# A row-gradient kernel: each store issued when the preceding store has landed, with semaphores by Tile

## Chip, cores, metric

One core of one Trainium2 chip. The metric is the device time of one execution in microseconds.

## The reference

The input is 8192 x 8192 float32, the output has the same shape:

```python
def reference(x: np.ndarray) -> np.ndarray:
    return np.gradient(x, axis=1)
```

Inside a row the result is half the difference of the right and left neighbour; at each row's two ends it is the plain difference of two neighbours. 268.44 MB must be read and as much written, with next to no arithmetic.

## The kernel before

The rows are cut into 32 sets of 256 rows (two rows per partition, 64 KB per partition, 8.39 MB per set). Three slots in SBUF hold sets in turn. For each set GpSimd computes the row ends (128x4), VectorE the inner part in place (one pass of 17.2 us), ScalarE puts the row ends in, and the set is stored. All loads and stores are issued by SyncE on one queue. Below, S_i is the store of set i and L_i its load.

```python
with tc.tile_critical():
    ...                                   # semaphores: ld[k], st[k] per slot, and others
    def load(i):
        k = i % NB                        # NB = 3
        ...
            nc.sync.wait_ge(st[k], 16 * st_n[k])       # slot free: S_(i-3) has landed
            parts = [(ld[k], 0, R)] if i < nsets - 1 else [(ld_rows[r], r, 1) for r in range(R)]
        for sem, r0, nr in parts:
            nc.sync.dma_start(out=slots[k][...], in_=x_sets[i, ...]).then_inc(sem, 16)
    ...
    def work(i, r0, nr, ready, placer, storer, sem):
        ...                               # VectorE pass, then the row ends by `placer`
        storer.wait_ge(*at)               # the set is ready
        storer.dma_start(out=out_sets[i, ...], in_=b[...]).then_inc(sem, 16)

    for i in range(NB):
        load(i)
    for i in range(nsets):
        ...                               # put_aside (row ends) and work for set i
        if i > 0 and i - 1 + NB < nsets:
            load(i - 1 + NB)              # L_(i+2), after S_i on the queue
    ...                                   # wait for all stores
```

So the queue carries L0 L1 L2 S0 S1 L3 S2 L4 S3 L5 ... The last set is loaded and worked on in two halves.

Some words used below: every transfer is shared out over 16 DMA engines, and each engine has its own share of the queue, its *ring*. A ring that runs empty is called dry. A transfer has *landed* when all 16 shares are done. A *turn* is the place where a load gives way to a store or a store to a load. *Tile* is the part of the kernel language that can place semaphores by itself.

## Time and profile before

| | before |
|---|---|
| median of 3 runs | 1251.41 us |
| span in the profile | 1249.5 us |
| share of the DMA queue | 99.5% |
| VectorE busy | 551.7 us, 44% |
| packets alone: (7936 x 2.418 + 512 x 1.213) / 16 | 1238.1 us |

Read it from the bottom: a transfer is cut into packets of 64 KB, each carried by one of 16 engines; if every packet took its usual time (2.418 us, or 1.213 us for a half packet) and no engine ever paused, the packets alone would take 1238.1 us. A packet that takes more than its usual time is called *long*; "long packets sum to" means the time above the usual, as the mean of the 16 engines.

### The profile page before, as it was taken

To read this page: it belongs to the slowest core of one execution; us is meant where nothing else is said; L and a number is where in the kernel's file an instruction comes from. 1 tells how busy PE (TensorE), PEld (TensorE's weight loads), DVE (VectorE), ACT (ScalarE), POOL (GpSimd) and SP (SyncE) were. 2 spreads that over 40 slices of the span, in tenths; PEclk is the share of its full clock that TensorE was granted. 3 is DMA by queue.
4 is the path that set the end of the run, shared out by engine and by line. 5 is a ranking of instruction groups with operands and counts; after the bars stand their busy time and mean duration, and the time that the engine had idled before them with its cause. 6 is when DMAs were issued, how large, how long until landed. Compare 5 with 4: busy or idle time off the path is not lost.

```text
span 1249.5 us, 225 instructions
## 1 busy us (share of the span) xinstructions
DVE 551.7 (44%) x35; ACT 7.4 (1%) x32; POOL 6.8 (1%) x37
## 2 busy tenths in 40 slices
DVE  2851455324553345533455333554335543355550
ACT  0000000000000000000000000000000000000000
POOL 0000000000000000000000000000000000000000
DMA  9999999999999999999999999999999999999997
GB/s 403 436 436 418 428 430 436 434 430 436 432 436 434 436 434 432 432 432 420 434 436 432 434 436 432 436 434 436 436 430 436 436 434 422 428 436 436 436 434 330
DMA packets 9505, 536.88 MB, mean 430 GB/s; under 512 B 1056, under 2 KB 1056, under 8 KB 1056
## 3 DMA queue, kind: packets, MB, share of 16 engines
q1 hardware_dynamic: 9504, 536.88, 99.5%
q14 instruction: 1, 0.01, 0.0%
HBM read 268.44 MB, written 268.44 MB: 430 GB/s over the span
## 4 chain that ended last, share of the span: by engine, by line
another core or an unknown queue 78%; DMA 15%; DVE 3%; POOL 0%; issue 0%; ACT 0%; SPq 0%
DMA slot<-in_x_dram 9%; DMA out_dram<-slot 7%; DVE slot L100 3%; POOL ends L82 0%; ACT slot L114 0%; DVE slot L114 0%; SPq L165 0%; SPq L42 0%
## 5 line engine op out<-in xcount | busy, mean ns | idle before, releaser
L100 DVE CUSTOM_DVE_ANT_0 slot<-slot 128x16382 f32<-128x16382 f32 (+1 forms) x33 | 551.3, 16707 | 666.5 <-POOL ends L82 666.5
L114 ACT COPY slot<-ends 128x4 f32<-128x4 f32 x31 | 6.1, 198 | 1179.8 <-DVE slot L100 1179.8
L82 POOL TENSOR_TENSOR ends<-slot 128x4 f32<-128x4 f32 (+1 forms) x33 | 6.6, 199 | 1202.2 <-DMA slot<-in_x_dram 1202.2
L114 ACT ACT_TABLE_LOAD x1 | 1.3, 1283 | 0.9 <-SPq L42 0.9
L114 DVE COPY slot<-ends 128x2 f32<-128x2 f32 x2 | 0.3, 170 | 0.1
L154 POOL MEMSET const-bfloat16-1.0<- 128x1 bf16 x1 | 0.1, 102 | 0.0
L154 POOL MEMSET const-uint8-127<- 128x1 uint8 x1 | 0.1, 102 | 0.0
L154 POOL MEMSET const-float32-0.0<- 128x1 f32 x1 | 0.1, 99 | 0.2 <-issue 0.2
L154 POOL MEMSET const-float32-1.0<- 128x1 f32 x1 | 0.1, 99 | 0.0
## 6 DMA issues: line engine op xcount, KB each, us to landing
slot<-in_x_dram SPq DMA_DIRECT2D x2, 4096.0 KB, 52.9
out_dram<-slot SPq DMA_DIRECT2D x2, 4096.0 KB, 29.5
slot<-in_x_dram SPq DMA_DIRECT2D x31, 58.4
out_dram<-slot SPq DMA_DIRECT2D x31, 40.3
```

Source lines behind the costliest of these rows:

```text
L82: nc.gpsimd.tensor_sub(out=ends[:, i, r0 : r0 + nr, :], in0=xin[:, :, 1 : m : m - 2], in1=xin[:, :, 0 : m - 1 : m - 2],),
L100: nc.vector._custom_dve(dve_ops.TENSOR_TENSOR_REDUCE_SUB_MAX, out=mid, in0=after, in1=before, s0=0.0, s1=0.5,),
L114: at = done(copy(out=to, in_=of), placed[placer])
L154: nc = _bacc.Bacc("TRN2", target_bir_lowering=False, num_devices=1)
```

## The change

Intent: a store is not put on the queue before the preceding store has landed, so that it goes "behind a load that has begun", with the load for the slot just freed right behind it. Beside that the hand-made semaphores in a critical section give way to Tile's, the row ends are placed by VectorE and GpSimd in place of ScalarE, and the last set is loaded in one piece (still worked on and stored in halves). The core of the diff, with cuts:

```diff
-    with tc.tile_critical():
-        ld = [nc.alloc_semaphore(f"ld{k}") for k in range(NB)]
...
+    with tc.manual_schedule():
...
-            placer.wait_ge(*at)
-            copy = nc.scalar.copy if placer is nc.scalar else nc.vector.tensor_copy
-            at = done(copy(out=to, in_=of), placed[placer])
-            storer.wait_ge(*at)
-            storer.dma_start(...).then_inc(sem, 16)
+                placer = nc.gpsimd if i % 5 in (1, 3) and not last else nc.vector
+                ins = placer.tensor_copy(out=res[:, :, 0 : m : m - 1], in_=ends[:, i, r : r + nr, :])
+                placed = chain(i, ins, halved)        # chain: keep only the named dependencies
+                ins = nc.sync.dma_start(out=out_sets[i, ...], in_=b[...])
+                stores[i] = chain(i, ins, placed)
+                if 2 <= i and not last:
+                    tc.add_manual_dep(ins.ins, stores[i - 1].ins.name, landed, reason="behind a load that has begun")
...
-            if i > 0 and i - 1 + NB < nsets:
+            if 1 <= i and i - 1 + NB < nsets:
                 load(i - 1 + NB)
```

More of the change, by code (lines that the diff above doesn't have):

```diff
@@ L40 @@
     ends = pool.tile([P, nsets, R, 2], f32, name="ends", tag="ends")
-    with tc.tile_critical():
-        ld = [nc.alloc_semaphore(f"ld{k}") for k in range(NB)]
-        st = [nc.alloc_semaphore(f"st{k}") for k in range(NB)]
-        ld_rows = [nc.alloc_semaphore(f"ld_row{r}") for r in range(R)]
-        st_rows = [nc.alloc_semaphore(f"st_row{r}") for r in range(R)]
-        aside = [nc.alloc_semaphore("aside"), 0]
-        halved = [nc.alloc_semaphore("halved"), 0]
-        placed = {
-            nc.vector: [nc.alloc_semaphore("placed_dve"), 0],
-            nc.scalar: [nc.alloc_semaphore("placed_act"), 0],
-        }
-        def done(ins, counter):
-            ins.then_inc(counter[0])
-            counter[1] += 1
-            return counter[0], counter[1]
-        ld_n, st_n = [0] * NB, [0] * NB
-        def load(i):
-            k = i % NB
-            if i < NB:
-                parts = [(ld[k], 0, R)]
-            else:
-                nc.sync.wait_ge(st[k], 16 * st_n[k])
-                parts = [(ld[k], 0, R)] if i < nsets - 1 else [(ld_rows[r], r, 1) for r in range(R)]
-            for sem, r0, nr in parts:
-                nc.sync.dma_start(
-                    out=slots[k][:, SH + r0 * m : SH + (r0 + nr) * m],
-                    in_=x_sets[i, :, r0 * m : (r0 + nr) * m],
-                ).then_inc(sem, 16)
-            ld_n[k] += 1
-        def put_aside(i, r0, nr, sem, count):
-            k = i % NB
-            xin = slots[k][:, SH + r0 * m : SH + (r0 + nr) * m].rearrange("p (t m) -> p t m", m=m)
-            nc.gpsimd.wait_ge(sem, count)
-            return done(
-                nc.gpsimd.tensor_sub(
-                    out=ends[:, i, r0 : r0 + nr, :],
-                    in0=xin[:, :, 1 : m : m - 2],
-                    in1=xin[:, :, 0 : m - 1 : m - 2],
-                ),
-                aside,
-            )
-        def work(i, r0, nr, ready, placer, storer, sem):
-            b = slots[i % NB]
-            c0, c1 = r0 * m + 1, (r0 + nr) * m - 1
-            mid = b[:, c0:c1]
-            after = b[:, SH + c0 + 1 : SH + c1 + 1]
-            before = b[:, SH + c0 - 1 : SH + c1 - 1]
-            nc.vector.wait_ge(*ready)
-            at = done(
-                nc.vector._custom_dve(
-                    dve_ops.TENSOR_TENSOR_REDUCE_SUB_MAX,
-                    out=mid,
-                    in0=after,
-                    in1=before,
-                    s0=0.0,
-                    s1=0.5,
-                ),
-                halved,
-            )
-            res = b[:, r0 * m : (r0 + nr) * m].rearrange("p (t m) -> p t m", m=m)
-            to, of = res[:, :, 0 : m : m - 1], ends[:, i, r0 : r0 + nr, :]
-            placer.wait_ge(*at)
-            copy = nc.scalar.copy if placer is nc.scalar else nc.vector.tensor_copy
-            at = done(copy(out=to, in_=of), placed[placer])
-            storer.wait_ge(*at)
-            storer.dma_start(
-                out=out_sets[i, :, r0 * m : (r0 + nr) * m],
-                in_=b[:, r0 * m : (r0 + nr) * m],
-            ).then_inc(sem, 16)
@@ new lines, with chain @@
+    landed = mybir.DependencyInfo(mybir.DependencyClass.Sync, mybir.DependencyReason.DATA)
+    loads, stores = [], [None] * nsets
+    in_front = {}
+    def chain(i, ins, *needed):
+        group, engine = f"slot{i % NB}", ins.ins.engine
+        keep = [o.ins for o in needed]
+        if in_front.get(engine, (None,))[0] == group:
+            keep.append(in_front[engine][1])
+        tc.declare_no_dep(ins.ins, group=group, keep=keep, reason="implied by the needed step")
+        tc.add_to_no_dep_group(group, ins.ins)
+        in_front[engine] = group, ins.ins
+        return ins
@@ L121, with load @@
+    def load(i):
+        b = slots[i % NB]
+        ins = nc.sync.dma_start(out=b[:, SH : SH + W], in_=x_sets[i])
+        loads.append(chain(i, ins, *([stores[i - NB]] if i >= NB else [])))
+    with tc.manual_schedule():
         for i in range(NB):
@@ L123 @@
         for i in range(nsets):
-            k = i % NB
-            if i < nsets - 1:
-                ready = put_aside(i, 0, R, ld[k], 16 * ld_n[k])
-                work(i, 0, R, ready, nc.scalar, nc.sync, st[k])
-                st_n[k] += 1
-            else:
-                for r in range(R):
-                    ready = put_aside(i, r, 1, ld_rows[r], 16)
-                    work(i, r, 1, ready, nc.vector, nc.sync, st_rows[r])
-            if i > 0 and i - 1 + NB < nsets:
+            b = slots[i % NB]
+            xin = b[:, SH : SH + W].rearrange("p (t m) -> p t m", m=m)
+            ins = nc.gpsimd.tensor_sub(
+                out=ends[:, i, :, :],
+                in0=xin[:, :, 1 : m : m - 2],
+                in1=xin[:, :, 0 : m - 1 : m - 2],
+            )
+            at = [chain(i, ins, loads[i])]
+            last = i == nsets - 1
+            nr = 1 if last else R
+            for r in range(0, R, nr):
+                c0, c1 = r * m + 1, (r + nr) * m - 1
+                ins = nc.vector._custom_dve(
+                    dve_ops.TENSOR_TENSOR_REDUCE_SUB_MAX,
+                    out=b[:, c0:c1],
+                    in0=b[:, SH + c0 + 1 : SH + c1 + 1],
+                    in1=b[:, SH + c0 - 1 : SH + c1 - 1],
+                    s0=0.0,
+                    s1=0.5,
+                )
+                halved = chain(i, ins, *at)
+                res = b[:, r * m : (r + nr) * m].rearrange("p (t m) -> p t m", m=m)
+                placer = nc.gpsimd if i % 5 in (1, 3) and not last else nc.vector
+                ins = placer.tensor_copy(out=res[:, :, 0 : m : m - 1], in_=ends[:, i, r : r + nr, :])
+                placed = chain(i, ins, halved)
+                ins = nc.sync.dma_start(
+                    out=out_sets[i, :, r * m : (r + nr) * m], in_=b[:, r * m : (r + nr) * m]
+                )
+                stores[i] = chain(i, ins, placed)
+                if 2 <= i and not last:
+                    tc.add_manual_dep(ins.ins, stores[i - 1].ins.name, landed, reason="behind a load that has begun")
+                at = [halved]
+            if 1 <= i and i - 1 + NB < nsets:
                 load(i - 1 + NB)
-        for r in range(R):
-            nc.sync.wait_ge(st_rows[r], 16)
-        for k in range(NB):
-            nc.sync.wait_ge(st[k], 16 * st_n[k])
 _INS = ['x']
```

## The prediction

> **What bounds the kernel now.** I read the page first: the slices, the DMA queues and the busy shares.
>
> ```profile
> DVE 551.7 (44%) x35; ACT 7.4 (1%) x32; POOL 6.8 (1%) x37
> ...
> DMA  9999999999999999999999999999999999999997
> GB/s 403 436 436 418 428 430 436 434 430 436 432 436 434 436 434 432 432 432 420 434 436 432 434 436 432 436 434 436 436 430 436 436 434 422 428 436 436 436 434 330
> ...
> q1 hardware_dynamic: 9504, 536.88, 99.5%
> HBM read 268.44 MB, written 268.44 MB: 430 GB/s over the span
> ```
>
> The compute engines are idle for more than half of the span; the one DMA queue keeps the 16 engines at work for 99.5% of it, and the rate hardly leaves 420 to 436 GB/s. The bytes are the least that the task allows (the input once, the output once). So the bound is the transfer rate. 536.87 MB at the best slices' 436 GB/s is 1231.4 us; the span is 1249.5. All that any change of order can win lies in those 18 us.
>
> To split the 18 us I read the packet records. A full packet (64 KB, 8 of them per engine in each 8.39 MB transfer) takes 2.418 us in more than nine of ten cases; 7936 of those and 512 half packets of 1.213 us, over 16 engines, are 1238.1 us. What is above that: 2.5 us before the first packet and 1.8 us from the last packet to the end of the span; on the engine that ends last 7.9 us of packets longer than their 2.418 us, on the ten least hurt only about 2 us. The rest is gaps of some 0.1 us per engine in all: **no DMA engine ever runs dry**. The long packets are 0.6 us in the first load, 1.1 us in the last packet of the third load, where the first store follows, and then some 0.1 to 0.7 us in the last packet of most loads on six of the sixteen engines, dying out after 816 us. They sit where a load gives way to a store.
>
> The second view is the timeline of two steady sets (start, length, what was issued or run):
>
> ```profile
> 138.57 0.33 SPq L116 DMA_DIRECT2D out_dram<-slot  x1
> 140.43 0.34 SPq L70 DMA_DIRECT2D slot<-in_x_dram  x1
> 159.97 0.20 POOL L82 TENSOR_TENSOR ends<-slot 128x4 f32<-128x4 f32 x1 [38.91 <-DMA slot<-in_x_dram]
> 160.20 17.23 DVE L100 CUSTOM_DVE_ANT_0 slot<-slot 128x16382 f32<-128x16382 f32 x1 [21.89 <-POOL ends L82]
> 177.46 0.20 ACT L114 COPY slot<-ends 128x4 f32<-128x4 f32 x1 [38.92 <-DVE slot L100]
> 177.68 0.33 SPq L116 DMA_DIRECT2D out_dram<-slot  x1
> 179.28 0.34 SPq L70 DMA_DIRECT2D slot<-in_x_dram  x1
> ```
>
> Call store i S_i and load i L_i. At 138.57 S_3 is issued, at 140.43 L_5, because S_2 has just landed and freed its slot. The next load to land (159.90) was L_4, issued at 101.63. So on each ring the order is S_2, L_4, S_3, L_5, S_4 ...; whenever a store lands, a whole load (19.3 us of work) still stands in front of the store just issued. The period is about 38.9 us (159.97 to 198.90 for the next set), against 16 x 2.418 = 38.7 us of pure packets.
>
> Third, the waits of the issuing queue (total, times, longest):
>
> ```profile
> SPq L116 <- ACT slot L114: 1090.5, 30, 38.3
> SPq L70 <- DMA out_dram<-slot: 73.9, 29, 21.6
> ```
>
> SyncE waits for the results before nearly every store (30 times, 36 us each), then for the preceding store to land before the load: without the two long waits of the start (the longest 21.6, the next about 19) (73.9 - 21.6 - 19.3) / 27 = 1.2 us each. The result is thus ready 1.2 to 1.9 us before the store ahead of it has landed. These waits cost no transfer time, since the rings are full meanwhile.
>
> **What the Trainium skill says.** DMA: Bandwidth & Descriptors, section "Bandwidth" (Where 436 GB/s comes from) puts the ceiling of the ports at 435.2 GB/s; the trace agrees, its best slices show 436. The same page, section "Queues, rings and completion order", says that each engine consumes its ring in order and that the engines finish independently; the landing order in the trace (S_2 at 140.4, L_4 at 159.9, S_3 at 179.3) agrees, and so do the six engines that end up to 6 us after the other ten. Its section "Anatomy of one DMA" says that DMA engines do not wait on semaphores, the wait lies on the issuing sequencer: an added wait therefore delays an issue, and takes bandwidth only if a ring empties. The trace has no empty ring before, so it can only be checked afterwards.
>
> **The change part by part.**
>
> Store issue. S_i (i from 2 to 30) now waits for S_(i-1) to have landed. In steady state it is issued 1.2 to 1.9 us later, say at 140.45 rather than 138.57, with the load right behind it (an issue takes 0.33 us). At that moment L_(i+1) has just begun and lasts 19.3 us, so S_i is on the rings some 17 us before it is needed even with 2 us taken for landing and issue. The engines' spread of up to 6 us still leaves 11 us. Cost 0, gain 0 on the rings.
>
> The start. S_0 (40.63) and S_1 (59.95) keep their time. L_3 still waits for S_0, 81.88. S_2, issued at 82.27 before, now waits for S_1 to land, 101.6, and L_4 follows it, also at 101.6 or 0.4 us later. L_3 is then on the rings until 120.8. No gap: 0 us.
>
> Who places the row ends. ACT's copies (31 of 198 ns) become 19 or so on VectorE (its own copies take 170 ns) and 12 on GpSimd (its small operation takes 200 ns). VectorE has 21.9 us idle per set. The placed row is wanted only when the preceding store lands, 1.5 us later: 0 us. ACT's table load of 1.28 us at the start goes, off the path.
>
> The last set. Its load is one transfer, not two halves with a semaphore each, so the first half cannot be started at 1199.3 but only when all has landed, 1209.0: the two halves then are ready at about 1209.3 + 8.7 = 1218.0 and 1218.2 + 8.7 = 1226.9, plus a copy of 0.2. On the rings S_30 runs from 1209 to 1228.4, and the first half store to 1238.0. The first half is issued 10 us before its turn, the second 11 us before. 0 us. Sixteen half packets of 1.213 us per engine become eight whole ones of 2.418: about 0.06 us less.
>
> Semaphores by Tile. Around the critical section there is little: the first load is issued at 0.95 us, and from the last landing to the end of the span are 1.8 us, mostly the barrier at the end, which both have. I give it plus or minus 0.5 us. Extra waits that Tile may add (reuse of its DMA semaphores, the shared row-end tile) would meet transfers or copies that are long done.
>
> Sum: 1251.4 - 0.06 +- 0.5 us. I choose 1250.5, leaning a little to faster since the only unexplained loss in steady state, the long packets, can shrink.
>
> **The rivals.**
>
> 1. The later issue changes the long packets at the load-to-store turn. For it: some 8 us of excess on the last engine, unevenly shared, and a turn of that kind can depend on what stands on the rings. Against it: at each turn S_i is on the ring in both kernels for over 15 us, in the same order. If all the excess went, the end would fall to about 1244; if the six engines kept paying 0.25 us until the end, the 12 remaining sets would add 3 us, 1254.
>
> 2. The new wait empties the rings: if a store landed late by its completion or if Tile made a load wait for more than its slot, each set would lose up to the 2 us between last packet and next issue, 29 x 2 = 58 us, 1309. Against it: a whole load is in front. It needs the wait for two stores back to become a wait for the load ahead, which the diff does not declare.
>
> 3. The last set, computed later, shows at the end. It has 10 us of slack by the numbers above; if S_30 were not in front, it would cost up to 9 us, 1260.
>
> 4. GpSimd holds back the next set by waiting for VectorE before its copy. It waits until 17.4 us after a load landed and the next load lands after 38.9: no. At the start the loads land every 19.3 to 20.3 us and the copy of set 1 falls about 2.5 us before load 2 lands: still no.
>
> **Range and chances.** The zero terms give 1251; rival 1 spans 1244 to 1254 but is improbable in its extremes; chip-to-chip and run scatter is below 1 us in the three times of before (1250.65 to 1251.45). So 1250.5, with 1245.0 to 1254.5 for 8 in 10. Faster by 2% would need 1226, below the 1231 us of the bytes at the best rate, so 0.01 is left for what I misread. Slower by 2% needs 25 us, that is rival 2 in half of the sets: 0.03.
>
> **What will show it.** Right: queue share still 99%, slices at 430 to 436; the store's issue line waits for the preceding store's landing about 29 times, the load right behind it by 0.3 to 0.5 us; periods of 38.6 to 39.2 us; the two last half stores landing 9.6 us apart with no gap after the one before. Wrong: slices below 420 in the middle, or landings of a load and the next store more than 20 us apart (rival 2); a last slice well under 330 GB/s (rival 3); or the six engines' long packets gone or doubled (rival 1), which would move the time by a few us and make my 0 for the order of issue wrong in size.

## The result, and the profile after

| | before | after |
|---|---|---|
| median (range) of 6 runs each | 1251.43 us (1250.65 to 1254.41) | 1250.82 us (1249.75 to 1254.98) |
| profiled span | 1249.5 us | 1247.7 us |

The ratio after/before is 0.9997, 95% interval 0.998 to 1.0014: the same.

The page of the kernel after, slices and queue:

```profile
DVE 554.8 (44%) x54; POOL 8.8 (1%) x48
...
GB/s 403 437 437 424 424 429 435 435 435 431 431 437 433 427 431 433 429 435 437 437 437 435 427 431 437 427 433 437 437 437 437 435 431 429 435 433 437 431 433 357
...
q1 hardware_dynamic: 9360, 536.88, 99.6%
```

The queue's share is 99.6% after 99.5%, the slices lie in the same band, and ScalarE has left the list. Parts of two steady sets in the timeline after (start, length, what):

```profile
138.44 0.19 POOL L93 COPY slot<-ends 128x4 f32<-128x4 f32 x1 [17.32 <-DVE slot L82]
140.42 0.34 SPq L95 DMA_DIRECT2D out_dram<-slot  x1
140.81 0.43 SPq L61 DMA_DIRECT2D slot<-in_x_dram  x1
160.17 0.20 POOL L71 TENSOR_TENSOR ends<-slot 128x4 f32<-128x4 f32 x1 [21.54 <-DMA slot<-in_x_dram]
160.41 17.22 DVE L82 CUSTOM_DVE_ANT_0 slot<-slot 128x16382 f32<-128x16382 f32 x1 [22.03 <-POOL ends L71]
177.66 0.17 DVE L93 COPY slot<-ends 128x4 f32<-128x4 f32 x1
179.55 0.33 SPq L95 DMA_DIRECT2D out_dram<-slot  x1
179.93 0.43 SPq L61 DMA_DIRECT2D slot<-in_x_dram  x1
```

Set 3 is ready at 138.63, but its store goes out at 140.42, when S_2 has landed (140.35), and L_5 follows 0.39 us later. Before, the store went at 138.57 and the load at 140.43. The store waits 1.85 us more, and the load now stands behind it, 0.38 us later than before. What SyncE waits for, after (total, times, longest):

```profile
SPq L95 <- DMA out_dram<-slot: 1082.2, 29, 38.8
SPq L95 <- DVE slot L93: 74.7, 3, 38.2
SPq L61 <- DMA out_dram<-slot: 21.5, 1, 21.5
```

The 1090.5 us that stood against "the copy of the row ends" before now stand against "the preceding store": 1082.2 us in 29 waits. This is a change of label. SyncE waits as long as before, and the rings are full while it does.

Where the 1.8 us between the two profiled spans come from can be read at the ends: the first load is issued at 0.74 in place of 0.95 us, and from the last landing to the last instruction it is 0.87 in place of 1.79 us. That makes 1.1 us. Part of it belongs to this one execution: before_with_wait and delay_6, which end like the kernel before, need 1.32 us there. The remaining 0.7 us lie in the long packets of the two executions, which differ from run to run (below).

### The profile page after: what moved, and what is told of

Read it like the earlier page. It is cut to its first block, busy times and chain, and to the rows that moved or that the text cites. A ratio compares the mean times of both kernels' runs of the same rounds, so it can differ in the third digit from the quotient of the medians.

```text
span 1247.7 us, 241 instructions
## 1 busy us (share of the span) xinstructions
DVE 554.8 (44%) x54; POOL 8.8 (1%) x48
## 3 DMA queue, kind: packets, MB, share of 16 engines
q1 hardware_dynamic: 9360, 536.88, 99.6%
## 4 chain that ended last, share of the span: by engine, by line
another core or an unknown queue 68%; DVE 18%; DMA 8%; issue 3%; POOL 1%; POOLq 0%
DVE slot L82 18%; DMA slot<-in_x_dram 5%; DMA out_dram<-slot 3%; POOL ends L71 0%; POOL slot L93 0%; DVE slot L93 0%; POOLq L129 0%
## 5 line engine op out<-in xcount | busy, mean ns | idle before, releaser
L71 POOL TENSOR_TENSOR ends<-slot 128x4 f32<-128x4 f32 x32 | 6.3, 198 | 991.5 <-DMA slot<-in_x_dram 991.5
L93 DVE COPY slot<-ends 128x4 f32<-128x4 f32 (+1 forms) x21 | 3.6, 171 | 0.7
## 6 DMA issues: line engine op xcount, KB each, us to landing
out_dram<-slot SPq DMA_DIRECT2D x31, 38.6
```

The source lines that it names most:

```text
L71: ins = nc.gpsimd.tensor_sub(out=ends[:, i, :, :], in0=xin[:, :, 1 : m : m - 2], in1=xin[:, :, 0 : m - 1 : m - 2],)
L93: ins = placer.tensor_copy(out=res[:, :, 0 : m : m - 1], in_=ends[:, i, r : r + nr, :])
```

## The experiments

Twelve runs. My theory: in front of every store a whole load (19.35 us of packets) stands on the rings, so the later issue costs nothing. Rivals: the wait costs something that another part of the change gives back; the turns from load to store, with their long packets, are affected; any delay of an issue counts in part.

The times, all against runs of the kernel before on the same chip:

| run | median, runs | ratio to before, 95% |
|---|---|---|
| before_with_wait | 1251.0, 5 | 0.999 (0.9977 to 1.0002) |
| after_without_wait | 1250.86, 5 | 0.9989 (0.9977 to 1.0002) |
| wait_for_load | 1316.01, 4 | 1.0513 (1.0497 to 1.0529) |
| one_turn (wrong result) | 1243.51, 4 | 0.9935 (0.9921 to 0.9948) |
| delay_6 | 1250.68, 4 | 0.9998 (0.9982 to 1.0014) |
| delay_12 | 1261.85, 2 | 1.008 (1.0062 to 1.0099) |
| delay_22 | 1442.36, 2 | 1.1531 (1.1509 to 1.1553) |
| last_whole | 1250.23, 5 | 0.9988 (0.9974 to 1.0001) |
| two_queues | 1251.56, 4 | 1.0006 (0.996 to 1.0051) |
| pairs | 1249.38, 6 | 0.9983 (0.9971 to 0.9996) |
| after_again | 1249.57, 5 | 0.9991 (0.9978 to 1.0004) |
| pairs_again | 1249.44, 5 | 0.9986 (0.9971 to 1.0) |

**before_with_wait: the wait alone.**

```diff
             storer.wait_ge(*at)
+            if 2 <= i < nsets - 1:
+                j = (i - 1) % NB
+                storer.wait_ge(st[j], 16 * st_n[j])
```

> The kernel before with one thing added: SyncE waits for the preceding store to land before each store from the third to the last but one. My theory (a whole load stands on the rings in front of each store, so the wait is free): ratio to before 0.998 to 1.002, queue share 99% or more, and the wait for the preceding store taking some 1080 us of SyncE's time. Rival (the new wait costs something and the semaphores by Tile, or the other engines for the copies, give the same back): over 1.003, 4 us or more.

The same. SyncE's waits show that the wait was in force:

```profile
SPq L118 <- DMA out_dram<-slot: 1082.5, 29, 39.6
```

**after_without_wait: everything but the wait.** The two lines with `add_manual_dep` are taken out of the kernel after.

> The changed kernel with the added wait for the preceding store taken out and the rest left (Tile's semaphores, row ends placed by VectorE and GpSimd, last load whole). My theory: ratio to before 0.998 to 1.002. Rival (the parts cancel): below 0.997, as what the rest gives would stand alone.

```profile
SPq L95 <- DVE slot L93: 703.2, 20, 38.3
SPq L95 <- POOL slot L93: 425.6, 12, 37.4
SPq L61 <- DMA out_dram<-slot: 73.3, 29, 21.6
```

SyncE waits for the results again, as in the kernel before, and the time is the same again (0.9989). The wait alone costs nothing and the rest alone gives nothing that the intervals, some 0.12% to each side, can show. So no two effects of several us cancel.

**wait_for_load: the same wait, moved to the load in front.** This empties the rings on purpose.

```diff
-                    tc.add_manual_dep(ins.ins, stores[i - 1].ins.name, landed, ...)
+                    tc.add_manual_dep(ins.ins, loads[i + 1].ins.name, landed, ...)
```

> The changed kernel, but each store waits for the load in front of it on the rings to land, not for the store in front of that load. My theory: now the rings run dry once a set, for the time from the last packet to the landing (0.34 us at the end of before) and from issue to first packet (1.0 us at its start): about 1.4 us x 29 = 40 us, 1292; if the engines, lined up afresh each set, also pay long packets at each turn from load to store as at the first one (about 1 us), up to 1321. Rival (the rings' filling doesn't matter, something else sets the pace): within 5 us of before.

64 us slower than before, within the range named. The timeline (the store, the next set's row ends, and the load):

```profile
614.43 0.33 SPq L95 DMA_DIRECT2D out_dram<-slot  x1
614.44 0.20 POOL L71 TENSOR_TENSOR ends<-slot 128x4 f32<-128x4 f32 x1 [40.94 <-DMA slot<-in_x_dram]
...
614.82 0.42 SPq L61 DMA_DIRECT2D slot<-in_x_dram  x1
...
655.57 0.33 SPq L95 DMA_DIRECT2D out_dram<-slot  x1
```

and its page:

```profile
GB/s 415 415 447 415 383 419 411 415 383 415 415 415 415 383 415 415 415 415 383 415 415 413 395 405 415 415 383 415 415 413 417 383 415 415 383 423 407 415 403 395
...
q1 hardware_dynamic: 9360, 536.88, 96.3%
```

The store and the row-end operation that waits for the load start at the same moment: the store now goes out when the load in front of it has landed. By the packet records no packet at all is under way for 37.8 us in sum, 1.3 us in each of 29 sets; and the packets that exceed their 2.418 us sum to 27.5 us per engine, against 4.1 before. Both terms of the forecast are there in size, but the second lies elsewhere than forecast: 22.8 of the 27.5 us are in packets of stores, most of them in a store's last packet, where it gives way to a load; before has 0.02 us in packets of stores. A wait of the very same kind, one transfer later on the ring, costs 5%.

**delay_12, delay_6, delay_22: how much later the store may go out.** From the kernel before with the added wait, ScalarE runs n copies of 128x1024 in a scratch tile after the landing of the preceding store, and the store waits for them.

```diff
+            if 2 <= i < nsets - 1:
+                j = (i - 1) % NB
+                nc.scalar.wait_ge(st[j], 16 * st_n[j])
+                for _ in range(n):                      # 12, then 6 and 22
+                    nc.scalar.wait_ge(*waited)
+                    done(nc.scalar.copy(out=idle[:, 0, :], in_=idle[:, 1, :]), waited)
+                storer.wait_ge(*waited)
```

> The kernel before with the added wait, and between the landing of the preceding store and this store's issue 12 copies of 128x1024 by ScalarE, about 12 to 14 us in all. Theory: the period of a set is the larger of 38.7 us of packets and 19.35 + 1.4 (issue to first packet 1.0, last packet to landing 0.34) + the delay; up to a delay of 17.9 us nothing is lost: 1248 to 1255 us. Rival (any delay of the issue counts, in part at least): 29 x 12 us gives up to 1600, a tenth of it 1285.

A miss: 1261.85 us, 10 us over before, where I had promised nothing lost. 3.3 us are my own doing: the scratch tile was cleared ahead of the critical section, and the first load went out at 4.25 in place of 0.95 us. The rest is in the packets: the long ones sum to 11.5 us per engine (before 4.1). The records date it. Up to about 500 us they are as before; from 600 us on they come on nearly all engines. And 6.4 of the 11.5 us lie in packets of stores, as they do where the rings run dry. In the timeline of that stretch

```profile
572.29 12.88 ACT L126 COPY idle<-idle 128x1024 f32<-128x1024 f32 x12 [1.58 <-DMA out_dram<-slot]
585.24 0.33 SPq L128 DMA_DIRECT2D out_dram<-slot  x1
...
592.61 0.20 POOL L86 TENSOR_TENSOR ends<-slot 128x4 f32<-128x4 f32 x1 [39.39 <-DMA slot<-in_x_dram]
```

the store goes out at 585.24 and its first packet can start about 0.8 us later (0.83 us from issue to first packet in each set of wait_for_load, where the rings were dry); the load in front lands at 592.54. But the slow engines land it. By then the fastest engine is 4.4 to 5 us ahead of the slowest in its packets, and reaches the end of that load at about 587.2, some 1 us after the store's packets can come; at 704 us the records show fast engines pausing for the store, for up to 0.4 us. In before the lead grows on, to 6.5 us; here it stays at 5.0 to 5.4 in the loads and 4.2 to 4.6 in the stores. So what is spare is not 17.9 us (19.35 - 1.4) but that less the engines' spread, some 12 us. My expectation for delay_12 had left out the spread, although the prediction had counted it.

The repair of the theory was tested on both sides, with the tile cleared out of the first load's way:

> As delay_12 with 6 copies, 6.5 us by what a copy took there (1.075 us with its wait), and the scratch tile cleared without holding up the first load. In delay_12 the store was issued 12.95 us after the landing, some 6 us before the end of the load in front, and from about 600 us, when the fast engines led the slow ones by 5 to 6 us, they reached the end of that load before the store's packets came; from then on all engines turned together and paid long packets. Revised theory: what is spare is 17.9 us less the engines' spread, 12 us: at 6.5 us nothing is lost, ratio 0.997 to 1.002, and long packets sum to 4 to 6 us. Rival (ScalarE's copies lengthen packets, or each us of delay costs its share): half of what delay_12 lost beyond its late start, 3 us or more, ratio 1.003 and long packets over 7 us.

> As delay_6 with 22 copies, 23.7 us. Past the limit: the period becomes 19.35 + 1.4 + 23.7 + 0.1 = 44.5 us in place of 38.7, 29 x 5.8 = 170 us more, and the engines turn together at every set, about 0.9 us of long packets each as in wait_for_load, 26 us: 1420 to 1450. Rival (the delay costs in proportion from the start, as 10 us for 12.95 us would have it): 1270.

Both came as expected: delay_6 0.9998 with 4.5 us of long packets, so the copies as such do no harm; delay_22 1442.36 us, inside 1420 to 1450. Two windows of 400 us, of delay_12 and of delay_6 (columns: window, length, busy time of VectorE, ScalarE and GpSimd, clock, DMA share, GB/s):

```profile
200.00:600.00 400.00, 179.40 (x11) 127.28 (x130) 2.18 (x11) 1.00 1.00 433
700.00:1100.00 400.00, 172.24 (x10) 130.49 (x134) 1.98 (x10) 1.00 1.00 428
```

```profile
200.00:600.00 400.00, 181.34 (x11) 64.63 (x70) 2.00 (x10) 1.00 1.00 433
700.00:1100.00 400.00, 177.17 (x11) 64.63 (x70) 2.20 (x11) 1.00 1.00 433
```

The delay of 12.9 us loses rate only in the second half, 428 for 433 GB/s, while the DMA share stays at 1.00: the engines are busy with longer packets, and their pauses sum to less than 1 us each in the whole run. So a late issue can cost time before the rings as a whole run dry. One set of delay_22, in the same columns, shows the other kind of loss:

```profile
575.80:621.30 45.50, 17.22 (x1) 23.20 (x24) 0.20 (x1) 1.00 0.87 369
```

There the share falls to 0.87: the rings stand empty for about 162 us in the whole run. What is not settled is why in delay_12 the packets grow once the fast engines come up to the end of the ring. My wording "all engines turned together" is not borne out to the letter, since a spread of 5 us remains.

**last_whole: the last set in one piece.** `nr = 1 if last else R` becomes `nr = R`.

> The changed kernel with the last set in one piece: one VectorE pass of 17.2 us and one store. From the trace after: last load lands at 1208.1, pass and copy until 1225.9, the store issued about then, while the store in front lands at 1227.5; from issue to first packet 1.0 us at the start of the kernel. My theory: it comes just in time, at most 0.5 us lost, ratio to before 0.998 to 1.001. Rival (halves in the last set are what keeps the end full): the last slice shows a gap of several us, 1255 or more.

The same (0.9988). The store goes out at 1225.54, the one in front lands at 1227.18. The records show that seven engines, long done with their share, stood idle for more than 5 us each waiting for it, while the slowest had no pause; all 16 then ended within 0.4 us of each other, at the time the slowest would have had anyway. Idle time of the fast engines at the end was free here. The halves of the last set thus gain nothing in the kernel after; in the kernel before, which loads it in halves too, this was not tried.

**one_turn: 32 loads, then 32 stores.** Wrong on purpose, without arithmetic.

```diff
+        for i in range(nsets):
+            ins = nc.sync.dma_start(out=b[:, SH : SH + W], in_=x_sets[i])      # waits for L_(i-3)
+        for i in range(nsets):
+            ins = nc.sync.dma_start(out=out_sets[i], in_=b[:, SH : SH + W])    # stale data
```

> Wrong result on purpose: all 32 loads first, each waiting only for the load three before it, then all 32 stores from the three slots, no arithmetic. Same bytes and packets, but one turn from load to store in place of 31. My theory (the long packets on some engines come from the turns): 1238.1 us of packets, 4.1 us at the ends, about 1.5 us in the first load and at the one turn: 1243 to 1245, ratio 0.993 to 0.995, and hardly any packet over 2.45 us after the start. Rival (they come from loading as such, or from the engines themselves): ratio 0.998 to 1.002 with the six engines behind as before.

1243.51 us, 8.5 us less than before; the queue line is

```profile
GB/s 405 439 439 439 412 433 439 439 439 439 424 420 439 439 439 439 420 424 439 439 439 439 435 410 439 439 439 439 439 433 412 439 439 439 439 439 431 414 439 405
...
q1 hardware_dynamic: 9216, 536.88, 99.9%
```

All engines end within 0.5 us, long packets sum to 2.0 us per engine. (A slice counts the packets that start in it, so 439 is no rate: 16 packets of 64 KB in 2.418 us are 433.7 GB/s.) From the first packet to the end of the last it is 1238.9 us, in the profiles of before 1245.4, after 1244.7 and 1243.3. So the spread of the engines, and 4 to 7 us of the slowest one, are gone when loads and stores do not alternate. The run left out the arithmetic too; but two_queues, which has it, has as few long packets, so the arithmetic alone does not make them. The single turn itself, with all engines in line, cost under 0.1 us, where I had expected some part of 1.5. Something more than a turn is needed.

**pairs: half the turns.** Without the added wait, the queue carries S S L L in place of S L S L.

```diff
-            if 1 <= i and i - 1 + NB < nsets:
-                load(i - 1 + NB)
+            if i % 2 == 1:
+                for j in (i - 1 + NB, i + NB):
+                    if j < nsets:
+                        load(j)
```

> The changed kernel without the added wait, and two stores then two loads on the queue in place of one of each, so half as many turns between loads and stores; in front of each issue still stands a whole transfer. If each turn costs the long packets, the engine that ends last loses 2 to 4 us less: ratio to before 0.997 to 0.9985, about 1248 us, and the summed excess of long packets falls from 4.1 to 4.7 us (mean of the engines) to about 3. Rival (the cost comes only when engines stand exactly in line, so the number of turns matters little): 0.999 to 1.001.

> The same file as pairs. If halving the turns is worth anything: ratio to before 0.997 to 0.999 and below that of after_again; if it was chance, no lower than after_again's.

> The changed kernel once more, for comparison with pairs on one chip: ratio to before 0.998 to 1.001.

pairs gave 0.9983, the size forecast. Beside the kernel after on one chip it is 0.9986 against 0.9991, and the intervals overlap almost wholly: a version that beats both kernels is not shown. The forecast sum of long packets (3 us) was missed as well: 3.9 and 4.0. Does the number of turns set the number of long packets? The records do not decide it. Counted from the third turn from load to store on, over packets longer than 2.45 us in the last packet of a load that a store follows: before has 118, pairs 119 and 95 at half as many turns, and none in the last packet of a load that a load follows. But the kernel after, executed twice, has 136 and 71, and after_without_wait, which differs from pairs by the order of the loads alone, has 263 (6.1 us per engine). Each is one execution. With the long packets the engines drift apart, by 4 to 8 us at the end (before 6.5, after 5.7 and 4.2 in two executions, pairs 5.0 and 6.1, after_without_wait 6.0, delay_6 8.2). In before the drift stops at about 840 us, in the second execution of after at about 400; in pairs and after_without_wait it still grows in the last 100 us, so that it comes to a limit of its own is not shown. This scatter of a few us, which also two executions of one kernel have, is as large as everything that separates before, after and pairs.

**two_queues: stores issued by ScalarE.** `nc.sync.dma_start` of the store becomes `nc.scalar.dma_start`, without the added wait.

> The changed kernel without the added wait and with the stores issued by ScalarE on its own queue, so that each engine has loads and stores at hand at the same time. If a turn costs because a load and a store follow each other on an engine, they now do so packet by packet, eight times as often: slower, 1260 to 1300 us, packets longer than 2.418 us as a rule. Rival (a turn costs only because all engines turn at once): long packets vanish, 1243 to 1247 us.

Inconclusive in time: the four runs took 1248.02, 1245.03, 1261.85 and 1255.1 us. The slow forecast (packets longer as a rule) is refuted by the profiled run of 1248.02: its packets keep 2.418 us, long ones sum to 2.1 us as in one_turn. What makes other executions 14 us slower has no profile and stays open. As a version it is no better on average.

## Why the prediction was right

It said 1250.5 us within 1245.0 to 1254.5; 1250.82 was measured. That the median lies this near is partly luck: the six runs of each kernel scatter over 4 to 5 us (one of after took 1254.98, outside the range), where the prediction had counted on less than 1 us, and its reason for leaning to faster, long packets that shrink, is not borne out by the profile (4.6 us after, 4.1 before). By its steps:

- *Store issue, cost 0.* Right, and shown from three sides: the wait added alone (0.999), taken away alone (0.9989), and moved until it does cost (wait_for_load, delay_22). The spare time was given as some 17 us, 11 after the engines' spread; the delays bracket the real limit between 6.5 and 12.9 us. Its rule that a wait takes bandwidth only if a ring empties is too narrow: in delay_12 no engine paused for more than 1 us in all, and still some 7 us were lost beyond the late start, in longer packets.
- *The start, no gap.* Right: S_2 went out at 101.30 and L_4 at 101.68, as L_3 (landed 120.86) was on the rings.
- *Row ends by other engines, 0.* Right: VectorE's copies took 171 ns, GpSimd's 190 ns, in steady state finished 1.6 to 1.8 us before they were wanted.
- *The last set, 0.* Right: the two half stores went out at 1217.34 and 1226.14 and landed at 1237.14 and 1246.82, 9.7 us apart behind a store landed at 1227.46. last_whole shows that even the halves are not needed.
- *Semaphores by Tile, plus or minus 0.5 us.* In the profile 1.1 us less at the two ends. I had said that both kernels have the barrier at the end; the critical section had one more of its own. It is not worth the whole 0.9 us, since before_with_wait and delay_6, with the same section, need 1.32 us from the last landing to the end where the profile of before has 1.79 and after 0.87. So some 0.45 us there and 0.2 us at the start, 0.65 us in all, are the section's: a little over the 0.5 given. Kernels without the wait or with it (0.9989, 0.9991, 0.9997) are in keeping with a gain of that size, but their intervals reach 1, so the times alone don't show it.
- *The first and last 2 us.* The prediction put 2.5 us before the first packet and 1.8 after the last. The records have 1.96 and 2.13. Its split also adds up to 1250.4 us, 0.9 more than the span, because on one engine a packet's record starts some 3 ns before the preceding one's ends, 1.6 us in all. Both slips have no effect on the forecast, which starts from the measured time.
- *Rival 1, long packets.* It was said that they could move the time by a few us but would not follow the order of issue. They follow the wait in no one direction: before and the kernel with the wait alone have 4.1 and 4.7 us per engine, after 4.6 and 3.8, after without the wait 6.1, the most. Each is one execution, and the times show no difference. Their cause is not found; shown is only that they come where whole loads and stores alternate on one queue (one_turn and two_queues have 2.0 and 2.1) and that the engines end 4 to 8 us apart.
- *The signs.* As listed: 99.6%, 29 waits, the load 0.39 us behind. The period was named too narrowly: up to 39.7 us in the first sets after, 39.4 before, in place of 38.6 to 39.2. The pattern of six late engines was not kept; in after the engines end in several groups between 1240.8 and 1246.5.
- *A section name.* The Trainium skill's words that the engines finish independently stand in the section "Why a DMA increments its semaphore by 16 and not by 1" of that page, not in the one that the prediction names for them.

## What to carry to other kernels

On a ring served in order, as here, ask of each issue how much work stands in front of it, less the landing, the issue and the spread of the engines: as long as that was positive here, waiting for more cost nothing and waiting for less gained nothing, whatever the totals in the list of waits say. The same kind of wait put one transfer later cost 5%, and a delay that came up to the limit cost more than the engines' pauses (7 us against 1). When one queue is busy 99.5% of the span, compare the packets' usual length times their number with the time first; here it left 1% for all reorderings together, about the size of the scatter between executions.

## What the Trainium skill lacked or had wrong

- "DMA: Bandwidth & Descriptors", section "Anatomy of one DMA", gives about 2.0 us as the fixed cost of a transfer, most of it the receipt of the last write (fitted on the GpSimd path). Here, on SyncE's queue with 8.39 MB transfers, from the last packet of the last store to its landing were 0.34 us, and a ring run dry cost 1.3 us from the last packet to the next transfer's first (wait_for_load: 0.40 us to the landing, 0.83 us from the issue to the first packet).
- The same page, section "Latency and other measured facts", gives about 600 ns to the first byte for SyncE's path. From issue to first packet were 1.0 us here at the start (0.95 to 1.96 before, 0.74 to 1.75 after) and 0.83 us in the 29 sets of wait_for_load; part of that may lie outside what the page counts.
- The same page, section "Why a DMA increments its semaphore by 16 and not by 1", says that the engines finish independently, but no page says how far they drift apart: 4 to 8 us over 1240 us of alternating loads and stores, 0.5 us with all loads first. From the first packet to the last this is 1243.3 to 1247.2 us against 1238.9, and the spread is taken from the slack of each issue.
- No page has a cost where loads and stores alternate: 0.1 to 1.1 us in a load's last packet where a store follows, rarer as the run goes on and the engines drift apart, and 0.7 us in each store's last packet where the rings had run dry before the store (wait_for_load).
- The rule of "DMA: Bandwidth & Descriptors", section "Rules for kernel authors", that issuing from several engines doesn't raise the bandwidth agrees in the mean (1.0006); no page tells of the scatter: 1245 to 1262 us with two queues, against 1251 to 1253 of the kernel before in the same rounds.
